# VectorE instead of GpSimd adds the squares of the norms; their one-column products and the factor's spreading stand later; Silu's table loads with the factor

## The chip, the cores and the metric

The kernel runs on one core of a Trainium2 chip, as one launch. The time is device microseconds, median over several executions. Five engines work side by side and wait for one another through semaphores: TensorE (PE in the profile, its weight loads are PEld), VectorE (DVE), ScalarE (ACT), GpSimd (POOL) and SyncE (SP), whose queue here issues nearly all transfers from memory. Each engine takes its instructions strictly in the order in which they were laid down.

## The reference

A trunk of two decoder layers over 256 tokens of width 1024, in float32. Everything starts from a norm, `y = h * rsqrt(mean(h*h) + 1e-6) * g`:

- layer 0: norm, projection to q, k, v and forget gates, forgetting attention (16 heads of 64), output projection, added to h;
- layer 1: the same with a block-sparse attention and a relative bias in place of the forget gates;
- in both: norm, `silu(u @ W1) * (u @ W2)` with 2816 columns each, projection back, added to h;
- in both: norm, `sigmoid(u @ Wg) * (p @ Wu)`, added to h ("the gate stage" below);
- one last norm.

Six of the seven norms stand in front of a projection. They are numbered 0 to 5 in the kernel: attention, feed-forward and gate stage of layer 0 (0, 1, 2), and of layer 1 (3, 4, 5).

## The kernel before

**Tiles.** h lies transposed, as 8 blocks of 128 channels by 256 tokens. A weight tile is 128x1024 (512 KB): eight 128x128 blocks. Each operand is split into a high part of the type fp32r and a low part, the rest, and each product is done as three: high by high, low by high, high by low (`mm3`, lines 91 to 93). For each weight tile SyncE issues its transfer into `raw` (6 buffers), ScalarE writes the high part `whi` (L155, L172, L135), VectorE subtracts to get the low part `wlo` (L156, L173, L138), 6 buffers each. One weight tile feeds 24 products (8 blocks, three products each) of 256 columns.

**Norms.** The factor of a norm is per token, and a projection is linear, so the kernel multiplies the raw h with the gain alone (`block`: high part on ScalarE, L189; low part on VectorE, L190), starts the projection with that, and applies the per-token factor to the projection's result. What the factor needs is done beside the projection: ScalarE squares h, two blocks of 128 channels at a time, in four parts (`square`, L197); GpSimd adds parts 1, 2 and 3 to part 0 as they come (L199, 128x512) and in `root` the two halves of the sum (L211, 128x256). TensorE then sums over the partitions: for each half of the tokens a product of the sum's 128x128 block with a column of ones (L214, `pr`; the one-column products). VectorE scales (L217), GpSimd takes the power -1/2 (L219, `col`), and in `spread` TensorE spreads the factor over partitions (L226) and ScalarE and VectorE copy it to `row` (L228, L229).

**Where the root stands.** TensorE's order is that of the program: the projection's products are written block by block of h, and `root` is called at a fixed place among them. In the feed-forward stages the first four weight tiles (f = 0, 1 and both halves) are worked block by block of h, 12 products a block, and `root` stands ahead of block 4 (L610); `spread` follows the next weight tile (L624). In the gate stage of layer 0 `root` stands behind the second of eight weight tiles, `spread` behind the third (L709, L712), and the results of the first four tiles are gated behind the fourth: VectorE multiplies with `row`, ScalarE takes the sigmoid, VectorE multiplies with `ut` and adds to h (L717 to L720), and the next norm's blocks and squares follow (`take`).

**Entries.** Where TensorE's first product on a weight tile is to start before the whole low part is written, the tile is either split in two on VectorE (`ENTRY`, L138: 128x256 and 128x768) or stored with its first block set apart by padding (`gapped`, 128x1080, 540 KB).

**Order.** A scheduler lays the instructions of VectorE, ScalarE, GpSimd and SyncE down by the program's order and by what each needs; TensorE's stays that of the program, but for a product or two.

## Time and profile before

| what | value |
|---|---|
| median of 3 runs | 663.9 us (662.43 to 664.05) |
| the profiled execution | 663.83 us |
| its span, first to last instruction | 661.7 us |
| mean granted TensorE clock in the span | 0.990 |
| TensorE busy, its weight loads busy | 644.9 us, 622.5 us |
| VectorE, ScalarE, GpSimd busy | 457.3 us, 373.1 us, 44.5 us |

Times in the views are microseconds from the span's start. "Busy" is the time in which an engine has an instruction under way; a row of the timeline gives start, duration, engine, line, operation, tiles written and read, shape, how many equal instructions were merged, and in brackets how long the engine sat idle before it and whom it waited for. Merged instructions overlap by a little, so two of 0.48 us can stand as 0.87. A matmul's own duration (0.28 us) holds its passage through the array; the step from one start to the next is what it costs in a row of them.

### The profile page before, as it was taken

How to read it: one execution, taken by the hardware profiler on the slowest of the kernel's cores; microseconds unless marked ns; L12 is line 12 of the kernel's file. 1: busy time of each engine (PE TensorE's matmuls, PEld its weight loads, DVE VectorE, ACT ScalarE, POOL GpSimd, SP SyncE). 2: the span in 40 equal slices, each digit the busy share in tenths (PEclk: the TensorE clock that was granted, in tenths of full speed). 3: DMA queues.
4: the chain of work that ended last, by engine and by line, in shares of the span. 5: the costliest groups of instructions: out<-in, count | busy, mean ns of one | idle time of the engine just before them, and what ended most of it. 6: DMA issues, size and time to landing. Idle time of an engine off the chain costs nothing. (4 is left out here: it accounts for less than half of the span.)

```text
span 661.7 us, 13228 instructions
## 1 busy us (share of the span) xinstructions
PE 644.9 (97%) x5375; PEld 622.5 (94%) x5375; DVE 457.3 (69%) x718; ACT 373.1 (56%) x632; POOL 44.5 (7%) x47
## 2 busy tenths in 40 slices
PE   9999999799999999999899999998999999999995
PEld 7899999799999999999888999998999999999985
DVE  6889775396666666668686788776766666666675
ACT  6686785274444445448565676754544444454663
POOL 1400000300000000002221000021000000000030
PEclk9999999799999999999899999999999999999999
DMA  8865533177776566665468555334755655666501
GB/s 339 293 205 191 161 129 128 66 281 258 240 241 199 194 193 207 194 198 181 142 205 309 190 165 158 106 130 143 239 198 193 193 193 194 195 211 189 187 1 63
DMA packets 35804, 124.14 MB, mean 188 GB/s; under 512 B 3904, under 2 KB 6176, under 8 KB 35744
## 3 DMA queue, kind: packets, MB, share of 16 engines
q1 hardware_dynamic: 35456, 122.88, 56.4%
q8 instruction: 42, 0.69, 0.4%
q10 hardware_dynamic: 288, 0.43, 0.2%
q14 instruction: 18, 0.15, 0.1%
HBM read 122.22 MB, written 4.22 MB: 191 GB/s over the span
## 5 line engine op out<-in xcount | busy, mean ns | idle before, releaser
L156 DVE TENSOR_TENSOR wlo<-raw,whi 128x1024 fp32r<-128x1024 f32 (+1 forms) x158 | 195.5, 1244 | 94.8 <-ACT whi L155 94.6
L155 ACT ACTIVATE whi<-raw 128x1024 fp32r<-128x1024 f32 (+1 forms) x157 | 164.6, 1055 | 133.1 <-issue 69.3
L91 PE MATMUL gu<-g,whi 128*128 128x256 f32 x704 | 196.2, 279 | 0.0
L92 PE MATMUL gu<-g,whi 128*128 128x256 f32 x704 | 195.9, 278 | 0.0
L93 PE MATMUL gu<-g,wlo 128*128 128x256 f32 x704 | 195.6, 278 | 0.0
L92 PEld LDWEIGHTS gu<-g,whi 128*128 128x128 f32 x704 | 133.5, 190 | 0.1
L91 PEld LDWEIGHTS gu<-g,whi 128*128 128x128 f32 x704 | 133.5, 190 | 0.0
L93 PEld LDWEIGHTS gu<-g,wlo 128*128 128x128 f32 x704 | 133.5, 190 | 0.0
L92 PE MATMUL fo<-fp,whi 128*128 128x256 f32 x352 | 97.5, 277 | 0.3
L93 PE MATMUL fo<-fp,wlo 128*128 128x256 f32 x352 | 97.4, 277 | 0.0
L91 PE MATMUL fo<-fp,whi 128*128 128x256 f32 x352 | 97.3, 276 | 0.0
L173 DVE TENSOR_TENSOR wlo<-raw,whi 128x1080 fp32r<-128x1080 f32 x41 | 53.3, 1300 | 39.5 <-ACT whi L172 38.9
L91 PE MATMUL pq<-g,whi 128*128 128x256 f32 x256 | 71.5, 279 | 0.0
L93 PE MATMUL pq<-g,wlo 128*128 128x256 f32 x256 | 71.0, 277 | 0.0
L92 PE MATMUL pq<-g,whi 128*128 128x256 f32 x256 | 70.9, 277 | 0.0
L92 PEld LDWEIGHTS fo<-fp,whi 128*128 128x128 f32 x352 | 66.2, 188 | 0.7 <-DVE fp L262 0.7
L91 PEld LDWEIGHTS fo<-fp,whi 128*128 128x128 f32 x352 | 66.1, 188 | 0.0
L93 PEld LDWEIGHTS fo<-fp,wlo 128*128 128x128 f32 x352 | 66.1, 188 | 0.0
L172 ACT ACTIVATE whi<-raw 128x1080 fp32r<-128x1080 f32 x41 | 45.1, 1103 | 36.6 <-PE gu L92 27.1
L199 POOL TENSOR_TENSOR sum<-sum,sq 128x512 f32<-128x512 f32 x18 | 27.2, 1512 | 564.9 <-issue 460.5
L91 PEld LDWEIGHTS pq<-g,whi 128*128 128x128 f32 x256 | 48.1, 188 | 0.6 <-issue 0.2
L92 PEld LDWEIGHTS pq<-g,whi 128*128 128x128 f32 x256 | 48.1, 188 | 0.1
(186 smaller groups left out, 1066.5 us busy)
## 6 DMA issues: line engine op xcount, KB each, us to landing
raw<-w SPq DMA_DIRECT2D x172, 512.0 KB, 3.7
raw<-w SPq DMA_DIRECT2D x41, 540.0 KB, 4.1
d<-d SPq DMA_DIRECT2D x4, 768.0 KB, 7.1
bias<-d SPq DMA_DIRECT2D x4, 512.0 KB, 5.6
out<-end SPq DMA_DIRECT2D x3, 256.0 KB, 2.0
hw<-wx SPq DMA_DIRECT2D x1, 640.0 KB, 6.7
hw<-xr SPq DMA_DIRECT2D x1, 640.0 KB, 8.6
raw<-w SPq DMA_DIRECT2D x2, 256.0 KB, 3.4
```

The costliest lines, as they stand in the source:

```text
L91: mm(o, ah, bh, start=start, stop=False, skip_group_check=True)
L92: mm(o, ah, bl, start=False, stop=False, skip_group_check=True)
L93: return mm(o, al, bh, start=False, stop=stop, skip_group_check=True)
L155: state["hi"] = nc.scalar.activation(hi[:, c], raw[:, c], AF.Copy)
L156: nc.vector.tensor_tensor(lo[:, c], raw[:, c], f32(hi[:, c]), op=ALU.subtract)
L172: nc.scalar.activation(ht, raw[:, 0:WW], AF.Copy)
L173: nc.vector.tensor_tensor(lt, raw[:, 0:WW], f32(ht), op=ALU.subtract)
L199: nc.gpsimd.tensor_tensor(self.sum, self.sum, sq, op=ALU.add)
```

## The change

- The four squared parts of a norm are kept (`parts`), and a new function `total` adds them on VectorE: part 1 to part 0, part 3 to part 2, both sums (128x512 each), and the two halves (128x256). GpSimd keeps the power alone. Before, GpSimd added each part as it came.
- In the first attention the squares are issued behind the high part of weight tile 3 and of weight tile 5, and `total` ahead of the forget gates' part.
- In the feed-forward stages `root` stands ahead of block 6 in place of block 4 of h, the padded entry of the first two weight tiles is that of block 6 and 7, and Silu's table is loaded there, by a one-column activation of the factor.
- In the gate stage of layer 0 `root` stands behind the third weight tile, `spread` and the gating of the first four tiles' results behind the fifth; all eight weight tiles are padded.
- In layer 1's projections one more tile is padded, and the split on VectorE is left to the first half of the first and third pair.

The diff:

```diff
--- before.py
+++ after.py
@@ -152,7 +152,7 @@
                 nc.vector.tensor_copy(hi[:, c], raw[:, c])
                 nm.block(i, hx[i])
             else:
-                state["hi"] = nc.scalar.activation(hi[:, c], raw[:, c], AF.Copy)
+                state["hi"] = state[f"hi{i}"] = nc.scalar.activation(hi[:, c], raw[:, c], AF.Copy)
             nc.vector.tensor_tensor(lo[:, c], raw[:, c], f32(hi[:, c]), op=ALU.subtract)
         return hi, lo
 
@@ -183,6 +183,7 @@
             self.both = work.tile([P, KT, 2, S], F32R, tag="act", name=f"g{n}")
             self.hi, self.lo = self.both[:, :, 0], self.both[:, :, 1]
             self.sum = work.tile([P, 2, S], F32, tag="row", name=f"sum{n}")
+            self.parts = [self.sum]
 
         def block(self, m, src):
             g = gn[:, self.n, m:m + 1]
@@ -191,12 +192,12 @@
 
         def square(self, b, *src):
 
-            sq = work.tile([P, 2, S], F32, tag="t2k", bufs=3, name=f"sq{self.n}_{b}") if b else self.sum
+            if b:
+                self.parts.append(work.tile([P, 2, S], F32, tag="t2k", bufs=3, name=f"sq{self.n}_{b}"))
+            sq = self.parts[b]
             src = src or (h[:, 2 * b:2 * b + 2],)
             for i, a in enumerate(src):
                 nc.scalar.activation(sq[:, i] if len(src) > 1 else sq, a, AF.Square)
-            if b:
-                nc.gpsimd.tensor_tensor(self.sum, self.sum, sq, op=ALU.add)
 
         def take(self, *bs):
 
@@ -205,10 +206,18 @@
                     self.block(m, h[:, m])
                 self.square(b)
 
+        def total(self):
+
+            a, b, c, d = self.parts
+            for x, y in ((a, b), (c, d), (a, c), (a[:, 0], a[:, 1])):
+                nc.vector.tensor_tensor(x, x, y, op=ALU.add)
+            self.parts = None
+
         def root(self):
 
             n = self.n
-            nc.gpsimd.tensor_tensor(self.sum[:, 0], self.sum[:, 0], self.sum[:, 1], op=ALU.add)
+            if self.parts:
+                self.total()
             self.pr = bank(f"pr{n}")
             for t in range(2):
                 mm(self.pr[:, S + t:S + t + 1], self.sum[:, 0, t * P:(t + 1) * P], ones, start=True, stop=True,
@@ -422,11 +431,14 @@
                         with tc.issue_after(state["hi"].ins), tc.issue_after(state["sum"].ins):
                             ahead.append(blocks())
             if layer == 0 and c == 1:
+                with tc.issue_after(state["hi3"].ins):
+                    nm.square(0, hx[0], hx[1])
+                    nm.square(1, hx[2], hx[3])
+                with tc.issue_after(state["hi5"].ins):
+                    nm.square(2, hr[:, 1:3])
+                    nm.square(3, hr[:, 3:5])
+                nm.total()
                 rest = mid(nm)
-                nm.square(0, hx[0], hx[1])
-                nm.square(1, hx[2], hx[3])
-                nm.square(2, hr[:, 1:3])
-                nm.square(3, hr[:, 3:5])
             if layer == 0 and c == 2:
                 ahead += [blocks(ENTRY), blocks()]
                 with tc.issue_after(nm.root().ins):
@@ -453,10 +465,10 @@
         def project(j, a):
             if ahead:
                 hi, lo = ahead.pop(0)
-            elif j > 2 and (j % 2 == 0 or layer and j == 5) and a == 0:
+            elif j > 2 and (j % 2 == 0 or layer and j == 5) and a == 0 or layer and j == 4:
                 hi, lo = gapped()
             else:
-                hi, lo = blocks(ENTRY if layer else ())
+                hi, lo = blocks(ENTRY if layer and j in (0, 2) and a == 0 else ())
             if a == 0:
                 pq[j] = bank(f"pq{layer}_{j}")
             bk = pq[j]
@@ -605,10 +617,11 @@
                 mm3(bks[f][:, a * S:(a + 1) * S], (wt[0][k], wt[1][k]), nm.k(k), start, k == KT - 1)
 
             if fs[0] == 0:
-                wts = {f: tuple(gapped(4 + a) if f == 0 else blocks() for a in range(2)) for f in fs}
+                wts = {f: tuple(gapped(6 + a) if f == 0 else blocks() for a in range(2)) for f in fs}
                 for k in range(KT):
-                    if k == 4:
+                    if k == 6:
                         nm.root()
+                        table(AF.Silu, nm.col[:, 0:1])
                     for f in fs:
                         for a in range(2):
                             step(f, a, wts[f][a], k, k == 0 and a == 0)
@@ -701,24 +714,28 @@
     def ple(layer, nm, ut, nx):
 
         bks = [[bank(f"pg{layer}_{hf}_{t}") for t in range(2)] for hf in range(2)]
+        def gates(hf):
+            for b in range(2):
+                sg = work.tile([P, 2, S], F32, tag="t2k", bufs=3, name=f"pgt0_{hf}_{b}")
+                at = slice(4 * hf + 2 * b, 4 * hf + 2 * b + 2)
+                nc.vector.tensor_tensor(sg, bks[hf][b].rearrange("p (m s) -> p m s", s=S), nm.row, op=ALU.mult)
+                nc.scalar.activation(sg, sg, AF.Sigmoid)
+                nc.vector.tensor_tensor(sg, sg, ut[:, at], op=ALU.mult)
+                nc.vector.tensor_tensor(h[:, at], h[:, at], sg, op=ALU.add)
+                nx.take(2 * hf + b)
+
         if layer == 0:
             for hf in range(2):
                 for c in range(4):
-                    wt = gapped() if c != 1 else blocks()
+                    wt = gapped()
                     cross(bks[hf], wt, (2 * c, 2 * c + 1), nm.k, 0, KT - 1, c == 3)
-                    if hf == 0 and c == 1:
+                    if hf == 0 and c == 2:
                         nm.root()
                         table(AF.Sigmoid, nm.col[:, 0:1])
-                    if hf == 0 and c == 2:
+                    if hf and c == 0:
                         nm.spread()
-                for b in range(2):
-                    sg = work.tile([P, 2, S], F32, tag="t2k", bufs=3, name=f"pgt0_{hf}_{b}")
-                    at = slice(4 * hf + 2 * b, 4 * hf + 2 * b + 2)
-                    nc.vector.tensor_tensor(sg, bks[hf][b].rearrange("p (m s) -> p m s", s=S), nm.row, op=ALU.mult)
-                    nc.scalar.activation(sg, sg, AF.Sigmoid)
-                    nc.vector.tensor_tensor(sg, sg, ut[:, at], op=ALU.mult)
-                    nc.vector.tensor_tensor(h[:, at], h[:, at], sg, op=ALU.add)
-                    nx.take(2 * hf + b)
+                        gates(0)
+            gates(1)
             return
 
         ht = ut[:, 2:4]
@@ -887,12 +904,12 @@
         wi = fw if i == 0 else mw
         wo = ar(fox_w_o)[0] if i == 0 else ar(moba_w_o)[0]
         seq += _rows(wi[:, 2 * D:3 * D])
-        seq += [_gapped(a) if n % 4 == 0 and n > 4 or i and n == 10 else a
+        seq += [_gapped(a) if n % 4 == 0 and n > 4 or i and n in (9, 10) else a
                 for n, a in enumerate(_cols(wi[:, :D], wi[:, D:2 * D]))]
         seq += [_gapped(_wide(wo, 2 * c, hf)) if (hf, c) in KICK else _wide(wo, 2 * c, hf)
                 for hf, c in ((0, 0), (1, 0), (0, 1), (1, 1), (0, 2), (1, 2), (0, 3), (1, 3))]
         a = _cols(fin[i][:, :DFF], fin[i][:, DFF:])
-        a[0:2] = [_gapped(a[n], 4 + n) for n in range(2)]
+        a[0:2] = [_gapped(a[n], 6 + n) for n in range(2)]
         for f in range(4, FT, 2):
             a[2 * f] = _gapped(a[2 * f])
         o = _rows(fout[i])
@@ -905,7 +922,7 @@
         seq += _rows(ar(ple_w_up)[i])
         seq += [_wide(fout[i], f, hf) for f, hf in ((FT - 2, 0), (FT - 4, 1), (FT - 2, 1))]
         a = [_wide(ar(ple_w_gate)[i], 2 * c, hf) for hf in range(2) for c in range(4)]
-        seq += a if i else [_gapped(t) if n % 4 != 1 else t for n, t in enumerate(a)]
+        seq += a if i else [_gapped(t) for t in a]
     xt = x[0].T.reshape(KT, P, S)
     wx = np.stack([np.concatenate([xt[k], seq[k]], axis=1) for k in (1, 2)])
     w = np.stack([np.pad(a, ((0, 0), (0, WW - a.shape[1]))) for a in seq[:1] + seq[3:]])
```

What moves, by the order of the instructions on VectorE. In the rows `h` is the residual stream, `g` the low part of its blocks, `wlo` a weight tile's low part, `sq` and `sum` the squared parts, `ms` the mean square; the line numbers of the changed kernel are 1 to 17 higher behind line 183.

VectorE in the feed-forward stage of layer 0, from the third residual to the first step of the factor, before:

```order
L156 TENSOR_TENSOR wlo_1666<-raw_1664,whi_1665 128x1024
L190 SCALAR_TENSOR_TENSOR g_172<-h,gx,g_172 128x256 x3
L294 TENSOR_TENSOR h<-hw,wo_1_1_1190 128x512
L138 TENSOR_TENSOR wlo_1717<-raw_1715,whi_1716 128x256
L138 TENSOR_TENSOR wlo_1717<-raw_1715,whi_1716 128x768
L190 SCALAR_TENSOR_TENSOR g_172<-h,gx,g_172 128x256 x2
L217 TENSOR_SCALAR ms_1607<-pr_1604 128x2
```

and changed:

```order
L156 TENSOR_TENSOR wlo_1667<-raw_1665,whi_1666 128x1024
L191 SCALAR_TENSOR_TENSOR g_172<-h,gx,g_172 128x256 x3
L303 TENSOR_TENSOR h<-hw,wo_1_1_1190 128x512
L213 TENSOR_TENSOR sum_173<-sum_173,sq_1_1478 128x512
L138 TENSOR_TENSOR wlo_1718<-raw_1716,whi_1717 128x256
L191 SCALAR_TENSOR_TENSOR g_172<-h,gx,g_172 128x256 x2
L213 TENSOR_TENSOR sq_2_1515<-sq_2_1515,sq_3_1522 128x512
L138 TENSOR_TENSOR wlo_1718<-raw_1716,whi_1717 128x768
L213 TENSOR_TENSOR sum_173<-sum_173,sq_2_1515 128x512
L213 TENSOR_TENSOR sum_173<-sum_173 128x256
L226 TENSOR_SCALAR ms_1631<-pr_1628 128x2
```

Four additions (L213) have come in between the fourth residual and the mean square, two of them behind a split of a weight tile; GpSimd's four of this norm are gone.

VectorE in the gate stage of layer 0, from the third residual to the mean square, before:

```order
L294 TENSOR_TENSOR h<-h,fo_1_0_1661 128x512
L173 TENSOR_TENSOR wlo_3998<-raw_3996,whi_3997 128x1080
L190 SCALAR_TENSOR_TENSOR g_1527<-h,gx,g_1527 128x256 x2
L294 TENSOR_TENSOR h<-h,fo_1_1_1662 128x512
L156 TENSOR_TENSOR wlo_4028<-raw_4026,whi_4027 128x1024
L190 SCALAR_TENSOR_TENSOR g_1527<-h,gx,g_1527 128x256 x2
L173 TENSOR_TENSOR wlo_4058<-raw_4056,whi_4057 128x1080
L217 TENSOR_SCALAR ms_3904<-pr_3901 128x2
```

and changed:

```order
L303 TENSOR_TENSOR h<-h,fo_1_0_1662 128x512
L173 TENSOR_TENSOR wlo_3972<-raw_3970,whi_3971 128x1080
L191 SCALAR_TENSOR_TENSOR g_1524<-h,gx,g_1524 128x256 x2
L303 TENSOR_TENSOR h<-h,fo_1_1_1663 128x512
L173 TENSOR_TENSOR wlo_4028<-raw_4026,whi_4027 128x1080
L191 SCALAR_TENSOR_TENSOR g_1524<-h,gx,g_1524 128x256 x2
L213 TENSOR_TENSOR sq_2_3823<-sq_2_3823,sq_3_3830 128x512
L173 TENSOR_TENSOR wlo_4058<-raw_4056,whi_4057 128x1080
L213 TENSOR_TENSOR sum_1525<-sum_1525,sq_2_3823 128x512
L213 TENSOR_TENSOR sum_1525<-sum_1525 128x256
L173 TENSOR_TENSOR wlo_4088<-raw_4086,whi_4087 128x1080
L226 TENSOR_SCALAR ms_3935<-pr_3932 128x2
```

The additions stand among the padded splits: the first just ahead of these rows, the second behind the last low parts, two behind one more split.

VectorE in the gate stage of layer 1, where the program's place of `root` is the same, before:

```order
L294 TENSOR_TENSOR h<-h,fo_1_1_5615 128x512
L156 TENSOR_TENSOR wlo_7897<-raw_7895,whi_7896 128x1024
L190 SCALAR_TENSOR_TENSOR g_5480<-h,gx,g_5480 128x256 x2
L156 TENSOR_TENSOR wlo_7903<-raw_7901,whi_7902 128x1024
L734 COPY ut_7610<-ht_1_7799 128x512
L734 COPY ut_7610<-ht_1_7811 128x512
L217 TENSOR_SCALAR ms_7827<-pr_7824 128x2
```

and changed:

```order
L303 TENSOR_TENSOR h<-h,fo_1_1_5606 128x512
L156 TENSOR_TENSOR wlo_7888<-raw_7886,whi_7887 128x1024
L191 SCALAR_TENSOR_TENSOR g_5467<-h,gx,g_5467 128x256 x2
L213 TENSOR_TENSOR sq_2_7738<-sq_2_7738,sq_3_7745 128x512
L156 TENSOR_TENSOR wlo_7894<-raw_7892,whi_7893 128x1024
L751 COPY ut_7601<-ht_1_7787 128x512
L751 COPY ut_7601<-ht_1_7799 128x512
L213 TENSOR_TENSOR sum_5468<-sum_5468,sq_2_7738 128x512
L213 TENSOR_TENSOR sum_5468<-sum_5468 128x256
L226 TENSOR_SCALAR ms_7818<-pr_7815 128x2
```

The last two additions stand behind the two copies of h's transposes (L751; L734 before).

## The prediction

> **What bounds the kernel now.** I read the page first, then TensorE's waits, then its timeline where the waits are, then the clock there.
>
> ```profile
> PE 644.9 (97%) x5375; PEld 622.5 (94%) x5375; DVE 457.3 (69%) x718; ACT 373.1 (56%) x632; POOL 44.5 (7%) x47
> ```
>
> TensorE is busy 97% of the span, so a change that leaves its products alone can win only what TensorE loses: its idle time, and time at a lower clock. Among TensorE's waits one row stands far above the rest:
>
> ```profile
> PE pr L214 <- POOL sum L211: 8.3, 3, 3.7
> ```
>
> Three times the one-column products waited for GpSimd's last addition, 8.3 us in all. TensorE's timeline around the three, in the two feed-forward stages and the gate stage of layer 0 between them:
>
> ```profile
> 119.36 0.28 PE L93 MATMUL gu<-g,wlo 128*128 128x256 f32 x1
> ...
> 119.70 0.28 PE L93 MATMUL gu<-g,wlo 128*128 128x256 f32 x1
> 123.63 1.01 PE L214 MATMUL pr<-first_line,sum 128*128 128x1 f32 x4 [3.65 <-POOL sum L211]
> ...
> 313.08 0.28 PE L93 MATMUL pg<-g,wlo 128*128 128x256 f32 x1
> 316.08 0.61 PE L214 MATMUL pr<-first_line,sum 128*128 128x1 f32 x4 [2.73 <-POOL sum L211]
> ...
> 446.47 0.28 PE L93 MATMUL gu<-g,wlo 128*128 128x256 f32 x1
> 448.69 0.61 PE L214 MATMUL pr<-first_line,sum 128*128 128x1 f32 x4 [1.94 <-POOL sum L211]
> ```
>
> The first two rows are three products apart: one costs 0.113 us. A stall is the step to the one-column products less 0.11: 3.82 us, 2.89 us and 2.11 us. Behind the first two the clock falls (the seventh column is the granted clock):
>
> ```profile
> 123.30:130.10 6.80, 6.47 (x30) 6.48 (x31) 0.16 (x1) 0.00 (x0) 0.98 (x2) 0.50 0.06 19
> 317.85:321.25 3.40, 3.40 (x19) 3.40 (x18) 0.24 (x1) 0.59 (x2) 0.80 (x1) 0.50 0.53 183
> ```
>
> 6.47 and 3.40 us of work ran at half clock, so half of each, 3.2 and 1.7 us, was lost. Behind the third stall no such stretch shows. The stalls with their clock cost 3.8+2.9+2.1+3.2+1.7 = 13.7 us.
>
> **Why GpSimd is late.** An addition on GpSimd is slow, and it holds up VectorE:
>
> ```profile
> 115.48 2.89 POOL L199 TENSOR_TENSOR sum<-sum,sq 128x512 f32<-128x512 f32 x2 [80.37 <-ACT sq L197]
> 121.26 1.51 POOL L199 TENSOR_TENSOR sum<-sum,sq 128x512 f32<-128x512 f32 x1 [2.88 <-ACT sq L197]
> 122.85 0.72 POOL L211 TENSOR_TENSOR sum<-sum 128x256 f32<-128x256 f32 x1
> 115.70 3.35 DVE L190 SCALAR_TENSOR_TENSOR g<-h,gx,g 128x256 fp32r<-128x256 f32 x3
> L190 DVE SCALAR_TENSOR_TENSOR g<-h,gx,g x40: 472/478/1520, 112.2 to 634.2; 128x256 fp32r<-128x256 f32 x40
> ```
>
> GpSimd's additions take about 1.5 us, and while two ran (115.48 to 118.37) three low parts took VectorE 3.35 us instead of 3 x 0.48. The longest one took 1.52 us against a median of 0.48, about one GpSimd addition. So the fourth residual, next on VectorE, is late by 1.9 us, and with it the last square.
>
> The Trainium skill, "SBUF — State Buffer", section "Who interferes with whom", says that a VectorE instruction with two inputs from SBUF and a GpSimd instruction that reads SBUF exclude each other for a whole instruction; these rows agree.
>
> **The change, part by part.** The nearest rows to VectorE's additions have the same shapes, both inputs in SBUF:
>
> ```profile
> L719 DVE TENSOR_TENSOR pgt<-pgt,ut x4: 679/682/684, 326.4 to 343.8; 128x512 f32<-128x512 f32 x4
> L743 DVE TENSOR_TENSOR ut<-ut,pgt x6: 425/426/684, 645.0 to 655.7; 128x256 f32<-128x256 f32 x4, 128x512 f32<-128x512 f32 x2
> ```
>
> A norm's additions cost VectorE 3 x 0.68 + 0.43 = 2.47 us; overlap with a neighbour can take 0.1 us off each, a handover between dependent ones adds a few hundredths.
>
> *Feed-forward, layer 0.* Rows of VectorE before:
>
> ```profile
> 118.98 0.68 DVE L294 TENSOR_TENSOR h<-hw,wo 128x512 f32<-128x512 f32 x1
> 119.58 1.28 DVE L138 TENSOR_TENSOR wlo<-raw,whi 128x256 fp32r<-128x256 f32 x2
> 120.78 0.87 DVE L190 SCALAR_TENSOR_TENSOR g<-h,gx,g 128x256 fp32r<-128x256 f32 x2
> ```
>
> The square of the fourth part is ready at most 1.6 us after the residual ends (119.66 to 121.26, where GpSimd starts on it). In the changed order: three low parts from 115.70, 1.4 us, to 117.1; residual 0.68, to 117.8; first addition, to 118.5; first quarter of the split, 0.4, to 118.9; two low parts 0.87, to 119.8 (the square is there by 119.4); second addition, to 120.5; the rest of the split 0.9, to 121.4; two additions 1.1, to 122.5; with the overlaps 121.9. TensorE now does blocks 4 and 5 first, whose low parts are ready by 117.1: 24 x 0.113 = 2.7 us from 119.81, to 122.5. The sum is there 0 to 0.6 us earlier, and both the stall and the half clock go: **-7.0**.
>
> *Gate stage, layer 0.* Rows of VectorE and GpSimd before:
>
> ```profile
> 307.16 1.64 DVE L173 TENSOR_TENSOR wlo<-raw,whi 128x1080 fp32r<-128x1080 f32 x1
> 308.73 1.92 DVE L190 SCALAR_TENSOR_TENSOR g<-h,gx,g 128x256 fp32r<-128x256 f32 x2
> 310.56 0.67 DVE L294 TENSOR_TENSOR h<-h,fo 128x512 f32<-128x512 f32 x1
> 314.38 1.65 POOL L211 TENSOR_TENSOR sum<-sum 128x256 f32<-128x256 f32 x1
> ```
>
> The residual moves from 310.56 by +0.68 (first addition) -1.05 (low parts back at 0.87) -0.35 (a padded split back at 1.28) to 309.8. Then residual, split, low parts, addition, split, two additions: 0.67+1.28+0.87+0.68+1.28+0.68+0.43 = 5.9, so 315.7 without overlaps, 315.2 with. TensorE finishes the third tile at 313.19+2.7 = 315.9. No stall: **-2.9**, and its half clock **-1.7**.
>
> *Feed-forward, layer 1.*
>
> ```profile
> 443.46 0.49 DVE L190 SCALAR_TENSOR_TENSOR g<-h,gx,g 128x256 fp32r<-128x256 f32 x1
> 447.85 0.79 POOL L211 TENSOR_TENSOR sum<-sum 128x256 f32<-128x256 f32 x1
> ```
>
> From the end of that low part, 443.95: an addition 0.68, three low parts 1.3, split 0.4, addition 0.68, split 0.9, additions 1.1: 449.0. TensorE wants it at 446.58+2.7 = 449.3, no longer at 446.6: **-2.1**.
>
> *Silu's table.* TensorE waits for the first gated product:
>
> ```profile
> 465.92 0.28 PE L91 MATMUL fo<-fp,whi 128*128 128x256 f32 x1
> 466.32 0.39 PE L92 MATMUL fo<-fp,whi 128*128 128x256 f32 x1
> L634 ACT ACT_TABLE_LOAD  x2: 1283/1283/1283, 139.6 to 461.7; - x2
> 132.87 1.23 DVE L156 TENSOR_TENSOR wlo<-raw,whi 128x1024 fp32r<-128x1024 f32 x1 [8.04 <-ACT whi L155]
> ```
>
> 0.40 us to the next product where 0.11 would do. The 1.28 us load on ScalarE leaves that chain for the stretch behind the norm in which, before, VectorE waited 8.04 us for ScalarE's next high part and ScalarE for a free buffer. Twice 0.3: **-0.6** (between 0 and -0.8).
>
> *Gate stage, layer 1.* Here `root` keeps its place and the additions fall behind the copies of the transposes.
>
> ```profile
> 635.66 1.75 DVE L156 TENSOR_TENSOR wlo<-raw,whi 128x1024 fp32r<-128x1024 f32 x1
> 637.34 1.27 DVE L734 COPY ut<-ht 128x512 f32<-128x512 f32 x2
> 637.43 0.50 PE L214 MATMUL pr<-first_line,sum 128*128 128x1 f32 x4
> ```
>
> Without GpSimd the split takes 1.22 and starts about 0.7 earlier, so the copies end near 637.4; two additions make it 638.5, and TensorE, which wants the sum at 637.7 (one product later than before), waits: **+0.8** (0 to 1.2).
>
> *Spreading, gate stage of layer 0.* It stands two tiles later, and the gating with it.
>
> ```profile
> 320.78 0.61 PE L226 MATMUL pr<-con,col 128*128 128x128 f32 x2
> 329.90 1.67 DVE L190 SCALAR_TENSOR_TENSOR g<-h,gx,g 128x256 fp32r<-128x256 f32 x4
> 334.96 0.40 PE L91 MATMUL v<-whi,g 128*128 128x512 f32 x1
> ```
>
> The first low part of the next norm ended 9.6 us after the spreading began. Layer 1's first product came 14.2 us after it; with three tiles between it is 3 x 2.7 + 0.3 = 8.5 us, and the low part is wanted two products later, at 8.9. TensorE waits: **+0.8** (0 to 1).
>
> *At nothing:* the first attention, whose additions replace slowed splits on VectorE; the later power, whose factor is wanted a weight tile (2.7 us) later; padding, some 0.06 us a tile on engines that wait; SyncE's queue, with the same number of transfers.
>
> Sum: -7.0-2.9-1.7-2.1-0.6+0.8+0.8 = -12.7, against the profiled execution's 663.83 (0.1 from the median): **651.1 us**.
>
> **The rivals.** The stretch from the spreading into layer 1:
>
> ```profile
> 322.00:350.00 28.00, 28.00 (x182) 25.41 (x182) 25.67 (x34) 18.26 (x27) 5.23 (x4) 1.00 0.60 193
> ```
>
> *The low parts are slow for another reason than GpSimd.* Then 3.35 stays, the fourth residual stays at 118.98, and the sum comes at 119.66+0.68+0.4+0.87+0.68+0.9+1.1 = 124.3, 1.8 late; in the gate stage 311.2+5.9 = 317.1, 1.2 late; layer 1 is taken as the same. Three waits of 4.2 us: 655.3. For it: the merged row shows no cause. Against: the excess is the length of a GpSimd addition. By the SBUF section above it falls. Chance 0.12.
>
> *VectorE binds between spreading and layer 1.* It is busy 25.67 of 28 us there, and the stretch shrinks while additions come in. If it falls 3 us behind, TensorE waits 3.0 instead of 0.8, and a halved clock, as behind the 2.89 us stall, takes 1.7: 655.0. Against: 2 us of that load are low parts and splits held up by GpSimd. Chance 0.10. The Trainium skill, "TensorE: Matmul & The Clock Gate", "Why this matters for your kernels", wants gaps over about 3 us (a window of 3.4) for the throttle; by it this case ends at 653.3. The 2.89 us stall halved the clock all the same.
>
> *The additions stand in the weights' way* (the slower side). If at each of six norms a weight's low part behind them comes late by all 2.47 us, TensorE pays 14.8 us and keeps the gains: 665.9; with the clock halved for 3.4 us twice, 669.3. It decides where a low part is done less than 2.47 us ahead of its use. Against: behind the norm VectorE was idle for 8.04 us, since the weights ahead were split. Chance 0.04.
>
> *The stalls move along with the products*, because the sum comes 2.7 us later too: 664. VectorE's rows above leave no room for that. Chance 0.03.
>
> **The numbers.** Forecast 0.71. Its own range: all new waits gone 649.5, a little less if more small steps vanish, to 653.5 if each of the three margins of 0 to 0.7 us is missed by as much. The range reaches to the two middle rivals: 648.8 to 656.5. A measurement of this kernel tells 0.3%, 2 us, from no change: faster 0.93, same 0.03, slower 0.04.
>
> **What would show it.** Right: TensorE's waits name no GpSimd addition; the one-column products follow a product without a gap over 0.3 us in those three places; no stretch at clock 0.5 between 10 and 640 us; no low part on VectorE over 0.6 us beside an addition; waits below 1 us in the gate stage of layer 1 and at layer 1's first product. Wrong: a wait over 2 us for VectorE's last addition, a half clock behind it, or TensorE waiting for a weight's low part.

## The result, and the profile after

The changed kernel takes **649.09 us** (median of 4 runs, 648.79 to 649.50) against 663.97 (4 runs, 662.43 to 664.87): a ratio of 0.978, 95% interval 0.976 to 0.980. The forecast was 651.1 us with a range of 648.8 to 656.5. The profiled execution took 648.79 us, its span is 647.0 us.

The engines' row and the clock row of the page, after:

```profile
PE 638.8 (99%) x5375; PEld 617.9 (96%) x5375; DVE 454.3 (70%) x731; ACT 374.6 (58%) x634; POOL 10.5 (2%) x23
...
PEclk9999999999999999999999999999999999999998
```

TensorE does the same 5375 instructions and is busy for 99% of the span. GpSimd's busy time is down from 44.5 to 10.5 us, VectorE's not up but down by 3.0 us, though it now does all the additions. All of TensorE's waits that the profile after names:

```profile
PE cold L110 <- PEq L954: 0.8, 1, 0.8
PE v L93 <- DVE g L191: 0.3, 1, 0.3
```

The row of 8.3 us is gone; what is left is the start of the program and 0.3 us at layer 1's first projection. TensorE's timeline at the three places, feed-forward of layer 0, gate stage of layer 0, feed-forward of layer 1:

```profile
121.90 0.28 PE L93 MATMUL gu<-g,wlo 128*128 128x256 f32 x1
122.02 0.50 PE L223 MATMUL pr<-first_line,sum 128*128 128x1 f32 x4
...
308.04 0.28 PE L93 MATMUL pg<-g,wlo 128*128 128x256 f32 x1
308.15 0.50 PE L223 MATMUL pr<-first_line,sum 128*128 128x1 f32 x4
...
436.99 0.28 PE L93 MATMUL gu<-g,wlo 128*128 128x256 f32 x1
437.11 0.50 PE L223 MATMUL pr<-first_line,sum 128*128 128x1 f32 x4
```

Each one-column product follows the product ahead of it by 0.11 or 0.12 us, the step of a row of products without a gap. VectorE's timeline in the first of the three, and then, by their line, the 40 low parts of the blocks of norms 1 to 5 (least, median and largest duration in ns):

```profile
115.19 1.27 DVE L191 SCALAR_TENSOR_TENSOR g<-h,gx,g 128x256 fp32r<-128x256 f32 x3
116.38 0.68 DVE L303 TENSOR_TENSOR h<-hw,wo 128x512 f32<-128x512 f32 x1
...
120.18 0.68 DVE L213 TENSOR_TENSOR sum<-sum,sq 128x512 f32<-128x512 f32 x1
120.89 0.42 DVE L213 TENSOR_TENSOR sum<-sum 128x256 f32<-128x256 f32 x1
```

```profile
L191 DVE SCALAR_TENSOR_TENSOR g<-h,gx,g x40: 470/478/485, 111.7 to 619.0; 128x256 fp32r<-128x256 f32 x40
```

Three low parts take 1.27 us, where they took 3.35 beside GpSimd; the sum is there at 121.31, 0.71 us ahead of its use. Of these 40 low parts none takes more than 0.485 us; before the longest took 1.52.

The span by stages, worked out from the starts of the first products that write the tile named (`pq` the projections to q and k, `gu` the feed-forward, `fo` its last projection, `pg` the gate stage, `pgl` the last 24 products of the kernel), in us:

| stage | before | after | difference |
|---|---|---|---|
| start to the first `pq` (layer 0's first norm in it) | 30.05 | 29.55 | -0.50 |
| to the first `gu` of layer 0 | 84.32 | 84.31 | 0 |
| feed-forward of layer 0, `gu` to `fo` | 29.43 | 22.53 | **-6.90** |
| `fo` to `pg`, layer 0 | 163.92 | 163.50 | -0.42 |
| gate stage of layer 0, to layer 1's first product | 27.24 | 22.68 | **-4.56** |
| layer 1's first product to `pq` | 22.53 | 23.14 | +0.61 |
| `pq` to the first `gu` of layer 1 | 83.52 | 83.10 | -0.42 |
| feed-forward of layer 1, `gu` to `fo` | 24.91 | 22.67 | **-2.24** |
| `fo` to `pg`, layer 1 | 164.26 | 163.84 | -0.42 |
| gate stage of layer 1, to `pgl` | 21.53 | 21.68 | +0.15 |
| `pgl` to the end | 9.97 | 10.05 | +0.08 |

The three stages in bold hold 13.70 of the 14.6 us.

### The profile page after: what moved, and what is told of

Its sections match the earlier page's. It is cut to its first block, busy times and chain, and to the rows that moved or that the text cites. A ratio compares the mean times of both kernels' runs of the same rounds, so it can differ in the third digit from the quotient of the medians.

```text
span 647.0 us, 13192 instructions
## 1 busy us (share of the span) xinstructions
PE 638.8 (99%) x5375; PEld 617.9 (96%) x5375; DVE 454.3 (70%) x731; ACT 374.6 (58%) x634; POOL 10.5 (2%) x23
## 4 chain that ended last, share of the span: by engine, by line
PE 95%; issue 3%; DVE 1%; ACT 0%; POOL 0%; POOLq 0%
PE gu L91 12%; PE gu L92 12%; PE gu L93 12%; PE fo L93 6%; PE fo L92 6%; PE fo L91 6%; PE pq L91 5%; PE pq L92 5%; PE pq L93 5%; PE v L406 3%; PE wo L91 2%; PE wo L92 2%; PE wo L93 2%; PE pp L535 2%; PE pg L91 1%
## 5 line engine op out<-in xcount | busy, mean ns | idle before, releaser
L156 DVE TENSOR_TENSOR wlo<-raw,whi 128x1024 fp32r<-128x1024 f32 (+1 forms) x166 | 200.9, 1216 | 85.2 <-ACT whi L155 79.9
L155 ACT ACTIVATE whi<-raw 128x1024 fp32r<-128x1024 f32 (+1 forms) x165 | 173.0, 1056 | 120.6 <-issue 51.6
L173 DVE TENSOR_TENSOR wlo<-raw,whi 128x1080 fp32r<-128x1080 f32 x44 | 56.3, 1280 | 42.0 <-ACT whi L172 41.3
L172 ACT ACTIVATE whi<-raw 128x1080 fp32r<-128x1080 f32 x44 | 48.5, 1104 | 39.0 <-PE gu L92 27.1
L93 PEld LDWEIGHTS pq<-g,wlo 128*128 128x128 f32 x256 | 48.1, 188 | 0.0
```

The lines of the kernel that those rows point to most:

```text
L93: return mm(o, al, bh, start=False, stop=stop, skip_group_check=True)
L155: state["hi"] = state[f"hi{i}"] = nc.scalar.activation(hi[:, c], raw[:, c], AF.Copy)
L156: nc.vector.tensor_tensor(lo[:, c], raw[:, c], f32(hi[:, c]), op=ALU.subtract)
L172: nc.scalar.activation(ht, raw[:, 0:WW], AF.Copy)
L173: nc.vector.tensor_tensor(lt, raw[:, 0:WW], f32(ht), op=ALU.subtract)
```

## The experiments

The theory was that GpSimd's additions came late and held VectorE, and that the one-column products' place 24 products further back was needed beside it. The kernels below take the change apart (E1, E2, E5, E6), put single costs back (E3, E4), move what still waits (E7 to E9), and put waits of a chosen length in (E10 to E12). Medians in us; "before" is its median in the same sitting.

| | kernel | time (runs) | before | ratio to before, 95% |
|---|---|---|---|---|
| E1 | VectorE adds, all places as before | 652.66 (652.48 to 652.80) | 664.74 | 0.981 to 0.984 |
| E2 | GpSimd adds, places as after (but the first attention's squares) | 652.43 (652.28 to 652.51) | 664.74 | 0.980 to 0.983 |
| E3 | after, with spare GpSimd additions | 664.05 (660.61 to 664.85) | 664.74 | 0.997 to 1.000 |
| E4 | after, with spare VectorE additions | 650.66 (650.27 to 650.78) | 664.74 | 0.978 to 0.981 |
| E5 | after, Silu's table not loaded early | 650.92 (650.67 to 651.22) | 664.28 | 0.979 to 0.982 |
| E6 | after, padding and splits as before | 649.19 (648.95 to 649.87) | 664.28 | 0.976 to 0.979 |
| E7 | after, spreading a weight tile earlier | 648.42 (647.95 to 649.08) | 664.28 | 0.975 to 0.978 |
| E8 | after, last root one step later | 648.66 (648.24 to 649.26) | 664.28 | 0.975 to 0.978 |
| E9 | E7 and E8 | 648.08 (647.94 to 648.15) | 663.76 | 0.974 to 0.977 |
| E10 | after, four steps more behind the sum | 651.45 (650.74 to 651.92) | 663.76 | 0.979 to 0.982 |
| E11 | six steps | 651.20 (650.79 to 652.41) | 663.76 | 0.979 to 0.982 |
| E12 | nine steps | 651.50 (651.32 to 652.02) | 663.76 | 0.979 to 0.982 |

### E1: the engine alone

The changed kernel with everything but `total` put back; the places in the feed-forward and gate stages, from the changed kernel to this one:

```diff
-                    if k == 6:
+                    if k == 4:
                         nm.root()
-                        table(AF.Silu, nm.col[:, 0:1])
...
-                    if hf == 0 and c == 2:
+                    if hf == 0 and c == 1:
                         nm.root()
                         table(AF.Sigmoid, nm.col[:, 0:1])
-                    if hf and c == 0:
+                    if hf == 0 and c == 2:
                         nm.spread()
```

> Only the engine of the additions is changed: VectorE adds the squared parts, but the root, the spreading, the gating, the padding, the first attention's squares and Silu's load stand as before. Theory A (the later place of the one-column products matters as much as the engine): in the changed kernel the sum was ready 0.70 us (feed-forward, layer 0), 0.75 us (gate stage, layer 0) and 0.71 us (feed-forward, layer 1) ahead of its use, and without the 24 products of 0.113 us that were put ahead of it (2.7 us) TensorE waits about 2.0 us in each of the three places for VectorE's last addition. With the Silu wait back (+0.8), the first attention and layer 1's projections back (+0.5 and +0.4) and layer 1's first product without its wait (-0.6): 649.1 + 6.0 + 0.8 + 0.9 - 0.6 = 656.2; 1.7 more for each of the three waits that halves the clock. Theory B (the engine alone matters, the later place only adds room): no wait over 0.5 us in the three places, 650 to 651.

Measured 652.66, between the two. TensorE's waits and its timeline in the feed-forward of layer 0:

```profile
PE pr L223 <- DVE sum L213: 1.7, 3, 0.8
```

```profile
120.93 0.28 PE L93 MATMUL gu<-g,wlo 128*128 128x256 f32 x1
121.82 0.35 PE L223 MATMUL pr<-first_line,sum 128*128 128x1 f32 x2 [0.62 <-DVE sum L213]
```

TensorE loses 0.8, 0.9 and 0.5 us in the three places (the steps less 0.11), not 2.0, and the clock is not halved. But the products do not stand where the program put them: between the first `gu` (114.21) and the one-column products lie 60 products, not the 48 of the kernel before, and 58 and 61 in the other two. With the sum added on VectorE the scheduler has laid 10 to 13 more products ahead by itself. So "the engine alone" cannot be had quite alone: moving the additions moved the products half way too. The lateness against the old place is what theory A said: 12 products of 0.113 us and the wait make 2.1 us in the first place.

### E2: the places alone

From the changed kernel (the squares of the first attention are put back to their old place as well, which is not shown):

```diff
                 nc.scalar.activation(sq[:, i] if len(src) > 1 else sq, a, AF.Square)
+            if b:
+                nc.gpsimd.tensor_tensor(self.sum, self.sum, sq, op=ALU.add)
+                self.parts[b] = None
...
-            a, b, c, d = self.parts
-            for x, y in ((a, b), (c, d), (a, c), (a[:, 0], a[:, 1])):
-                nc.vector.tensor_tensor(x, x, y, op=ALU.add)
+            nc.gpsimd.tensor_tensor(self.sum[:, 0], self.sum[:, 0], self.sum[:, 1], op=ALU.add)
```

> The reverse: GpSimd adds the squared parts as before (the first attention's squares stand as before too), and everything else is as in the changed kernel: one-column products one step of 2.7 us later, spreading later, padding, Silu's load. Theory A (a place 2.7 us later is most of the gain): the sum, ready at 123.57 in the kernel before on a TensorE that then wants it at about 122.0, is 1.1 to 1.6 us late in the feed-forward of layer 0, 0 to 0.3 us late in the gate stage, in time in the feed-forward of layer 1; no clock is halved; with the first attention's 0.5 us lost 650.5 to 651.5. Theory B (GpSimd's hold on VectorE is most of it): the low parts stay at 3.35 us for three and the sum comes later still with the later place of the splits around it; waits of 2 to 3 us stay with at least one half clock behind them: 655 or more.

Measured 652.43. VectorE, GpSimd and TensorE in the feed-forward of layer 0, and TensorE at layer 1's first norm:

```profile
115.62 3.35 DVE L191 SCALAR_TENSOR_TENSOR g<-h,gx,g 128x256 fp32r<-128x256 f32 x3
...
122.79 0.72 POOL L214 TENSOR_TENSOR sum<-sum 128x256 f32<-128x256 f32 x1
...
122.33 0.28 PE L93 MATMUL gu<-g,wlo 128*128 128x256 f32 x1
123.57 0.61 PE L224 MATMUL pr<-first_line,sum 128*128 128x1 f32 x4 [0.96 <-POOL sum L214]
...
343.23 0.49 PE L224 MATMUL pr<-first_line,sum 128*128 128x1 f32 x3 [1.30 <-POOL sum L214]
```

The hold is there to the hundredth (3.35 us for three), and still theory A holds in the feed-forward stages: the wait is 1.13 us in layer 0, 0.4 in the gate stage, none in layer 1's feed-forward, and no clock is halved. The 1 us beyond that theory's range is a place that it left out: at layer 1's first norm, whose blocks and squares follow the gating that now stands later, the sum comes 1.5 us late.

E1 and E2 together, each against before in its own sitting: the engine saves 12.1 us, the places 12.3 (with Silu's load and the padding, which by the table of stages are 0.8 and 0.4 us of it), both 14.9. They are **two remedies for one lateness**, each nearly enough, not two terms of a sum. In the feed-forward of layer 0 the stage goes from 29.43 to 23.39 (E1), 23.79 (E2) and 22.53 us (both).

### E3: the hold itself

```diff
                     self.block(m, h[:, m])
                 self.square(b)
+                if b:
+                    if b == 1:
+                        self.spare = work.tile([P, 2, S], F32, tag="e", bufs=4, name=f"spare{self.n}")
+                    two = f32(self.hi[:, 2 * b:2 * b + 2])
+                    nc.gpsimd.tensor_tensor(self.spare, two, two, op=ALU.add)
```

> The changed kernel with one spare GpSimd addition (128x512, two inputs from SBUF, its result read by nobody) behind each of the squared parts 1 to 3 of norms 1 to 5, where GpSimd's additions stood before; no engine waits for it by a semaphore except for its buffer. Theory (GpSimd's addition holds VectorE's instructions with two inputs from SBUF): in the feed-forward of layer 0 the longest low part goes from 0.48 us to about 1.5 us, the sum is late by about 1 us beyond its margin of 0.70, and the time rises by 1 to 3 us, to 650 to 652. Rival (the low parts were slow for another reason, such as the place of their inputs or the splits ahead): low parts stay at or below 0.6 us and the time at 649.1 +- 0.5.

Measured 664.05: the whole gain is gone, 15.0 us where 1 to 3 were expected. The low parts of the norms' blocks, and then the timeline of VectorE, GpSimd and TensorE in the feed-forward of layer 0:

```profile
L191 DVE SCALAR_TENSOR_TENSOR g<-h,gx,g x40: 471/481/1346, 112.1 to 632.1; 128x256 fp32r<-128x256 f32 x40
```

```profile
115.52 2.84 DVE L191 SCALAR_TENSOR_TENSOR g<-h,gx,g 128x256 fp32r<-128x256 f32 x3
119.82 1.66 DVE L191 SCALAR_TENSOR_TENSOR g<-h,gx,g 128x256 fp32r<-128x256 f32 x2
...
114.78 2.91 POOL L212 TENSOR_TENSOR spare<-g 128x512 f32<-128x512 f32 x2 [79.84 <-ACT g L190]
...
122.23 0.28 PE L93 MATMUL gu<-g,wlo 128*128 128x256 f32 x1
124.15 0.58 PE L228 MATMUL pr<-first_line,sum 128*128 128x1 f32 x4 [1.64 <-DVE sum L218]
```

The mechanism is shown: a GpSimd addition that nobody waits for makes the low part beside it up to 1.35 us long; the longest before took 1.52. The Trainium skill, "SBUF — State Buffer", section "Who interferes with whom", has it so: two VectorE inputs from SBUF and a GpSimd instruction that reads SBUF shut each other out. These rows agree. The size was off. The expectation counted one low part held; here the two groups of three and two take 1.57 + 0.79 us more, so the sum comes, counted from the stage's first product, 2.37 us later than in the changed kernel, and its margin hides 0.7 of that. And it counted one place; the same happens in the gate stages (+2.0 and +4.1 us as stages), at layer 1's first norm (+0.9) and in layer 1's feed-forward (+3.8). Three times a halved clock follows, 1.7 us each and so 5.1 of the 15.0 us: behind the waits of the two feed-forward stages, which are read below, and behind a step of 2.79 us in the gate stage of layer 1.

### E4: what VectorE has to spare

```diff
                 nc.vector.tensor_tensor(x, x, y, op=ALU.add)
+            for y in (b, d, c, a[:, 1]):
+                nc.vector.tensor_tensor(y, y, y, op=ALU.add)
             self.parts = None
```

> The changed kernel with VectorE's additions doubled: four spare ones a norm (three of 128x512 and one of 128x256, 2.47 us a norm, 14.8 us over six norms), whose results nobody reads. About two of the four stand between the true ones, so the sum itself comes about 1.4 us later at each norm. Theory (VectorE has room there; only the margin of 0.7 us ahead of the one-column products counts): 1.4 - 0.7 = 0.7 us in each of four or five places, some 3 to 4 us in all, 652 to 653, and no TensorE wait for a weight's low part. Rival (the additions stand in the way of the weights' low parts, each microsecond of VectorE behind a norm costs TensorE one): 14.8 us more, about 664.

Measured 650.66, 1.6 us above the changed kernel for 14.8 us more on VectorE, and half of what the theory expected (3 to 4 us): in the feed-forward stages the sum came only 0.2 us later than in the changed kernel, counted from the stage's first product, not 1.4, and the margin of 0.7 us hid that. TensorE in the gate stage of layer 0:

```profile
309.32 0.58 PE L225 MATMUL pr<-first_line,sum 128*128 128x1 f32 x4 [0.32 <-DVE sum L213]
```

The step to it is 0.59 us, so 0.5 us is lost here; the first attention loses 0.6, layer 1's first norm 0.3, the feed-forward stages nothing (22.53 and 22.66 us). No wait names a weight's low part. The rival in which additions stand in the weights' way is out: nine tenths of what VectorE does behind a norm costs TensorE nothing.

### E5 and E6: Silu's table, and the padding

E5 takes out the line `table(AF.Silu, nm.col[:, 0:1])`. E6 puts back, from the changed kernel:

```diff
-            elif j > 2 and (j % 2 == 0 or layer and j == 5) and a == 0 or layer and j == 4:
+            elif j > 2 and (j % 2 == 0 or layer and j == 5) and a == 0:
...
-                hi, lo = blocks(ENTRY if layer and j in (0, 2) and a == 0 else ())
+                hi, lo = blocks(ENTRY if layer else ())
...
-                    wt = gapped()
+                    wt = gapped() if c != 1 else blocks()
```

> The changed kernel without the one-column activation that loads Silu's table with the factor, so that the load falls into the first gated product of each feed-forward stage again. Theory: TensorE waits 0.4 us twice ahead of the last products with fo, +0.8 us: 649.9. Rival (the load is hidden anyway, or the early load pushes ScalarE's high parts back): within 0.2 us of 649.1.

> The changed kernel with the padding and the splits on VectorE in layer 1's projections and in the gate stage of layer 0 as before. Theory: layer 1's projections got 0.42 us shorter through these; TensorE's small waits there come back: +0.4 us, 649.5, and nothing in the gate stage of layer 0. Rival (they are shorter because the norm's additions no longer hold VectorE): no change.

E5 measured 650.92, 1.8 above the changed kernel. TensorE at the first products with `fo`, in E5 and then in the changed kernel:

```profile
136.64 0.28 PE L91 MATMUL fo<-fp,whi 128*128 128x256 f32 x1
137.05 0.39 PE L92 MATMUL fo<-fp,whi 128*128 128x256 f32 x1
```

```profile
136.39 0.28 PE L91 MATMUL fo<-fp,whi 128*128 128x256 f32 x1
136.50 0.28 PE L92 MATMUL fo<-fp,whi 128*128 128x256 f32 x1
```

The wait comes back, and the stage behind it is 0.60 us longer in layer 0 and 0.42 in layer 1. That is 1.0 of the 1.8 us, a little more than the 0.8 expected. The profiled execution has 0.8 us more between `pgl` and the end, and 0.4 us more ahead of the first `gu` of layer 0, which E10's execution has too, with the load in its early place; whether either belongs to the edit was not settled. E6 measured 649.19, no difference that can be told, yet its trace has the theory's term: from `pq` to `gu` of layer 1 it takes 83.52 us as before, against 83.10, and its gate stage of layer 0 is as after. 0.42 us is below what the time can show, since the start up to the first `pq` alone lies between 29.3 and 30.1 us in nine executions of kernels that are the same up to there.

### E7, E8 and E9: what still waits

E7, spreading and first gating behind the fourth tile, and E8, the last root a step later; E9 is both:

```diff
-                    if hf and c == 0:
+                    if hf == 0 and c == 3:
                         nm.spread()
                         gates(0)
...
-            if c == 1:
+            if c == 2:
                 nm.root()
                 table(AF.Sigmoid, nm.col[:, 0:1])
```

> The changed kernel with the spreading and the first gating in the gate stage of layer 0 one weight tile earlier (behind the fourth, as the gating was before, not behind the fifth). Theory: the 0.61 us that TensorE lost at layer 1's first products goes, because gating, adding and the next norm's blocks start 2.7 us earlier: 648.5. Rival (the factor is not there yet, TensorE or VectorE waits for it, or the additions now meet the gating on VectorE): 0 to +1 us.

> The changed kernel with the one-column products in the gate stage of layer 1 one step (2.7 us) later. Theory: TensorE's remaining wait there for VectorE's last addition (about 0.2 us) goes and nothing waits for the factor in its place: 648.9. Rival (the factor comes too late for the gating at the end of the layer, which nothing follows but the last norm): +1 to +3 us.

> The changed kernel with both small moves: the spreading and first gating of the gate stage of layer 0 one weight tile earlier, and the one-column products of the gate stage of layer 1 one step later. Each alone measured 0.7 and 0.4 us below the changed kernel's 649.1, with 0.61 us gone at layer 1's first product and 0.18 us in the last gate stage. Theory (the two waits are independent): 649.1 - 0.8 = 648.3. Rival (the later root of the last gate stage only paid by chance of the last transfer): 648.5 to 648.9.

Layer 1's first products in the changed kernel, and then in E7:

```profile
322.80 0.40 PE L92 MATMUL v<-wlo,g 128*128 128x512 f32 x1
323.51 0.50 PE L93 MATMUL v<-whi,g 128*128 128x512 f32 x1 [0.31 <-DVE g L191]
```

```profile
322.57 0.40 PE L92 MATMUL v<-wlo,g 128*128 128x512 f32 x1
322.81 0.39 PE L93 MATMUL v<-whi,g 128*128 128x512 f32 x1
```

E7's wait is gone and nothing else became longer: the stage from there to `pq` is 22.53 us again, -0.61. In E8 the one-column products follow without a wait, and the last gate stage is 0.14 us shorter. E9 measured 648.08 us (the theory said 648.3), with all runs below all runs of the changed kernel (which were made in another sitting): a ratio of 0.975 to before. The factor was there in time one weight tile earlier; its later place was not needed for the gain.

### E10 to E12: waits of a chosen length

In E10, with 6 and 9 steps in place of 4 in E11 and E12:

```diff
             if self.parts:
                 self.total()
+            if n in (1, 4):
+                for _ in range(4):
+                    nc.vector.tensor_tensor(self.sum[:, 0], self.sum[:, 0], self.sum[:, 0], op=ALU.max)
```

> The changed kernel with a wait of a chosen length put ahead of the one-column products of the two feed-forward stages: four VectorE instructions on the sum (the larger of the sum and itself, 128x256, about 0.46 us each with their handover), so the sum is 1.84 us later, 1.14 us beyond its margin of 0.70. Theory W (the clock is halved for 3.41 us after any stretch of 3.41 us, on a grid that runs on from the start, in which TensorE is busy less than about a third): 1.14 us and the one-column products leave at least half of each stretch busy, so no clock is halved: 649.1 + 2 x 1.14 = 651.4 in every execution, all within 1 us. Theory L (the length of the wait decides, from about 1.8 us): 651.4 too. Theory S (any wait of TensorE at a one-column product is followed by a loss of 1.7 us): 654.8.

> The same with six such instructions: waits of 2.06 us in the two feed-forward stages. Theory W: with the one-column products, TensorE idles 2.5 us; a stretch of 3.41 us holds 2.2 us or more of that in (3.41 + 2.5 - 4.4)/3.41 = 0.44 of the positions. So executions of 653.2, 654.9 and 656.6 us, with mean clocks that step by 0.0026 with them, about 654.7 in the mean. Theory L (length decides, 1.8 us is enough): 656.6 in every execution; if only from 2.9 us: 653.2 in every execution.

> The same with nine such instructions: waits of 3.44 us. Theory W: 3.9 us idle, halved in (3.41 + 3.9 - 4.4)/3.41 = 0.85 of the positions, and a second stretch follows where the wait reaches far into the first: 649.1 + 6.9 = 656.0, and 1.7 more for each halved stretch, mostly two of them or more: 659.4, executions from 657.7 to 661. Theory L: 659.4 in every execution, within 0.5 us. In both, VectorE's 4.1 us more behind each of the two norms cost nothing beyond the waits.

E10 is at its 651.4, but E11 and E12 are there as well, at 651.2 and 651.5: no theory foresaw that. VectorE and TensorE of E12 in the feed-forward of layer 0:

```profile
121.25 4.10 DVE L223 TENSOR_TENSOR sum<-sum 128x256 f32<-128x256 f32 x9
...
124.12 0.28 PE L92 MATMUL gu<-g,whi 128*128 128x256 f32 x1
125.50 0.47 PE L226 MATMUL pr<-first_line,sum 128*128 128x1 f32 x3 [1.10 <-DVE sum L223]
```

The nine steps took 4.10 us as planned, but TensorE waited 1.27 us, not 3.44: 92 products stand ahead of the one-column products, where the changed kernel has 72 (E10 has 74, E11 81). The scheduler had seen VectorE's chain and laid TensorE's products around it. So these three did not make the waits that they were for, and do not decide between the theories on the clock. They say something else: a lateness that the scheduler reckons with cost 1.0 to 1.4 us a place, at all three lengths.

### The halved clock, from the traces at hand

Three of E3's waits have one length, 1.92, 1.94 and 1.91 us from the product ahead. Two were followed by a halved clock, one was not. The second and the third (the first is shown above):

```profile
311.84 0.28 PE L93 MATMUL pg<-g,wlo 128*128 128x256 f32 x1
313.78 0.47 PE L228 MATMUL pr<-first_line,sum 128*128 128x1 f32 x3 [1.66 <-DVE sum L218]
...
443.66 0.28 PE L93 MATMUL gu<-g,wlo 128*128 128x256 f32 x1
445.57 0.58 PE L228 MATMUL pr<-first_line,sum 128*128 128x1 f32 x4 [1.64 <-DVE sum L218]
```

Its stretches of 3.41 us, counted from 122.12 (duration, busy time of each engine with its instructions, then the granted clock):

```profile
122.12:125.53 3.41, 1.77 (x16) 1.60 (x15) 2.01 (x4) 0.00 (x0) 0.53 (x1) 1.00 0.44 130
125.53:128.94 3.41, 3.41 (x19) 3.41 (x18) 0.59 (x1) 1.88 (x3) 0.18 (x1) 0.50 0.06 24
309.85:313.26 3.41, 2.27 (x20) 2.07 (x19) 3.38 (x6) 2.74 (x4) 0.25 (x1) 1.00 0.44 156
313.26:316.68 3.42, 2.90 (x25) 2.93 (x26) 2.77 (x4) 1.24 (x2) 1.61 (x1) 1.00 0.72 228
442.97:446.38 3.41, 1.77 (x16) 1.60 (x15) 2.58 (x5) 0.00 (x0) 0.00 (x0) 1.00 0.27 82
446.38:449.80 3.42, 3.42 (x18) 3.42 (x18) 0.00 (x0) 0.89 (x2) 0.70 (x1) 0.50 0.18 72
```

These two halved stretches begin 94.0 lengths of 3.4133 us apart (125.53 and 446.38), and in each of the fourteen traces all changes of the granted clock lie whole numbers of that length apart (35 of it from 6.06 to 125.53 here). Laid on that grid, the first and third wait lie whole in one stretch, which leaves TensorE 1.77 us of busy time, and the next stretch is granted half; the second (311.95 to 313.78) is cut by the boundary at 313.26, both parts stay at 2.27 us or more, and the clock stays full. The kernel before, on its own grid:

```profile
314.43:317.84 3.41, 1.76 (x15) 1.76 (x16) 2.13 (x3) 1.54 (x2) 2.47 (x2) 1.00 0.54 184
317.84:321.26 3.42, 3.42 (x19) 3.42 (x18) 0.25 (x1) 0.60 (x2) 0.81 (x1) 0.50 0.53 182
444.14:447.55 3.41, 2.60 (x23) 2.41 (x22) 3.41 (x4) 1.53 (x4) 2.98 (x2) 1.00 0.00 0
447.55:450.96 3.41, 2.27 (x19) 2.27 (x20) 1.53 (x3) 0.00 (x0) 1.71 (x3) 1.00 0.47 154
```

The wait of 2.11 us behind which the prediction found no such stretch is cut at 447.55; that of 2.89 us left a stretch with 1.76 us busy.

The busy time alone does not decide. The stretch ahead of the second halved one of the kernel before, and one at the end of E10:

```profile
123.28:126.70 3.42, 3.07 (x14) 3.08 (x15) 0.16 (x1) 0.00 (x0) 1.00 (x2) 0.50 0.11 40
641.47:644.88 3.41, 1.59 (x15) 1.39 (x13) 2.49 (x7) 2.07 (x5) 1.02 (x2) 1.00 0.00 0
```

The first shows 3.07 us busy, at half clock, and the next stretch (126.70 to 130.11) is halved as well; the second shows 1.59 us, less than the 1.76 and 1.77 above, and the next one is at full clock. What separates them is the work that starts in a stretch: 10 products of 256 columns in the first, 12 in the second, against 9 and 10 in the two of E3 that were followed by a halved one and 11 in that of before (the four one-column products not counted). So it is in all fourteen traces once the clock is full behind the start: behind a stretch in which products of 11 times 256 columns or fewer start the next one is halved, with 12 times 256 or more (in E2, at layer 1's first norm, six of 512) it is not. This is read from the traces; no run was made to test it.

The Trainium skill, "TensorE: Matmul & The Clock Gate", section "What's actually happening", has a window of 3413 ns that runs freely and does not start with the kernel; the grid agrees with it to 0.1%. The same page's "Why this matters for your kernels" asks for gaps below about 3 us; a wait of 1.8 us inside one window was enough here.

The executions bear it out: in E3 those with a mean clock of 0.989 took 663.9 to 664.9 us, those at 0.991 or 0.992 took 662.2 to 662.7, the one at 0.993 took 660.6. The steps are about the 1.7 us that one halved stretch costs. The changed kernel has no wait long enough, and its runs lie within 0.7 us where those of before spread over 2.4.

## Why the prediction was right

**The three stages were right to 0.15 us.** Forecast -7.0, -4.6 and -2.1 us, measured -6.90, -4.56 and -2.24. The steps behind them hold one by one: the low parts went from 3.35 to 1.27 us, the sum was ready at 121.31 for a use at 122.02 (forecast 121.9 for 122.5, in a program that starts the stage 0.5 us later), no one-column product waited, no clock was halved between 10 and 640 us.

**What the sum did not say** is that the two halves of the remedy overlap. It gave the gain of each place to the edit as a whole, which was right; whoever had split it into "the engine" and "the place" would have been wrong, since each alone gives 12 of the 14.9 us (E1, E2). Each cures the lateness down to waits of at most 1.5 us a place, and no clock was halved behind those.

**The scheduler's part was mis-stated.** The text ahead of the prediction says that TensorE's order stays the program's but for a product or two. E1 moved 10 to 13 products and E12 20 by itself. That also changes how the kernel before is read: its one-column products stood at the program's place, 48 products in, and waited 3.82 us, while a chain on VectorE of 4.10 us was met with a wait of 1.27. That the scheduler's reckoning lacks the hold of GpSimd on VectorE would explain this. E3, which puts only the hold back, points the same way, since its one-column products stay at the program's 72 products and wait 1.8 us; but it is argued from these, not shown.

**Terms that were mis-sized**, 1.9 us together with the scatter of start and end:

- *Gate stage, layer 1*: +0.8, measured +0.15. VectorE's rows before the products:

```profile
621.12 1.28 DVE L751 COPY ut<-ht 128x512 f32<-128x512 f32 x2
622.31 0.68 DVE L213 TENSOR_TENSOR sum<-sum,sq 128x512 f32<-128x512 f32 x1
623.03 0.42 DVE L213 TENSOR_TENSOR sum<-sum 128x256 f32<-128x256 f32 x1
```

  The order of events was as forecast, copies and then two additions in 1.1 us, but counted from the first `pg` the copies end 0.1 us earlier (7.1 against 7.2), and 28 products stand ahead of the one-column ones, where before had 24 and the forecast took 25; a step of 0.35 us in place of 0.23 is all that is left.
- *First attention*: "at nothing", measured -0.50 in all, of which the 0.28 us between its one-column products and `pq` (6.70 to 6.42) is steady: E1 and E2, with the squares at the old place, have 6.64, E5 to E12 have 6.42. The rest is the scatter of the start.
- *Padding*: "at nothing", measured -0.42 in layer 1's projections. It is the padding and the splits there, not the additions: E1 and E6, without them, have 83.52 us, and E2, with them and with GpSimd's additions, has 83.10.
- *Silu's table*: -0.6, measured -0.84. The forecast took the step to the next product alone (0.40 less 0.11); the product behind it came late as well. E5, which takes out this load alone, gives 1.02.
- *Spreading*: +0.8, measured +0.61, at the product foreseen.

Two figures of the prediction do not come out of their own terms, and neither enters the forecast. Three margins of 0.7 us make the upper end of its own range 653.2 (651.1 + 2.1), not 653.5. And the excess of the longest low part is not the length of a GpSimd addition: it is 1.04 us (1.52 less 0.48), while it is the whole 1.52 us that comes near the addition's 1.51.

**The rivals.** *Low parts slow for another reason*: fell with 470/478/485 ns after and with E3. *VectorE binds between spreading and layer 1*: a wait of 0.6 us came, not 3; E4 put 2.47 us more there for 0.3. *The additions stand in the weights' way*: E4, 1.6 us for 14.8. *The stalls move along*: no. The halved clock behind a wait of 3 us, which the second rival used, would not have been certain: it depends on where the wait falls on the grid.

## What to carry to other kernels

A GpSimd instruction that reads SBUF costs what it does to VectorE, not its own time: look for a VectorE instruction whose longest duration is far above its median and near that of a GpSimd instruction (here 1.52 us against 0.48, beside additions of about 1.5), and put such work on VectorE if it has room (here 2.47 us a norm, nearly free). When a consumer waits, an earlier producer and a later place for the consumer are two cures for one lateness, so don't add their gains. A TensorE wait of about 2 us can cost 1.7 us more or nothing, by where it falls; keep it short, and read the halved stretches of several executions before you put a price on it.

## What the runs showed of the hardware that was not expected

- The clock is granted on a grid of 3.413 us that runs on through the kernel. 1.9 us steps in E3 halved it twice and left it alone once; what separates the stretches of all fourteen traces behind the start is the work that starts in one of them, up to 11 products of 256 columns (the next one halved) against 12 or more (not), while the busy time does not (1.59 us not, 1.76 and 3.07 us halved).
- The spread of a kernel's times goes with it: in E3 a mean clock of 0.993 goes with 660.6 us, 0.989 with up to 664.9.
- Fifteen GpSimd additions of 1.2 us each that nobody waits for, on an engine that is busy for 5% of the span, cost 15 us of 649.
